# Rotating 96 images by 90 degrees: which bytes of the last group are stored first

## The chip, the core and the metric

The kernel runs on one core of a Trainium2 chip. The metric is the device time of one execution in microseconds (us). Three runs of the kernel before the change took 123.16, 123.51 and 123.54 us, median 123.51.

## What is computed

The input is float32 of shape (32, 3, 256, 256), that is 96 images of 256 x 256, 25.17 MB. The output is each image turned clockwise by a quarter:

```python
def reference(x):
    return np.rot90(x, k=-1, axes=(-2, -1)).astype(np.float32)
```

No arithmetic is done on the values. Every byte is read from device memory (HBM) once and written once, 50.33 MB in all, and between the two it has to change both its partition and its place in the row.

## The kernel before

**Groups.** The 96 images are cut into four groups of 2, 2, 4 and 4 slabs (`sizes`, line 39). A slab is 16 rows of 256 numbers on each of the 128 partitions: 16 KB on a partition, 2 MB in all. Each group has a tile of its own in on-chip memory (`groups`, lines 41 to 44), so no group waits for another's buffer. `E` is the length of a slab's row on a partition, 4096 numbers, `Q` is half of it, and `W` is one image row, 256 numbers.

**Loads.** All loads and stores are DMAs issued by SyncE (SP), in the order of the text. Lines 58 to 69 load the groups in order. The last load is cut in two (lines 66 and 67), and the first of its halves is remembered as `mark`.

**Turning.** VectorE (DVE) transposes with `turn` (line 82): a stream transpose turns blocks of 32 x 32 numbers between partitions and free dimension, and its access patterns, with negative steps, put the reversed order in. ScalarE (ACT) copies with `copy` (line 85). `keep` (line 73) holds the order on each engine as written. A group is turned in place. For that, the output rows of a slab are split in `low` (rows 0 to 7 of its 16, the lower 8 KB) and `high` (rows 8 to 15, the upper 8 KB), and the positions inside a row likewise, which makes four quadrants `A` (low, low), `B_` (high, low), `C_` (high, high) and `D` (low, high), with the row half first (line 118). For groups 2 and 3 there are two turns (t = 0, 1) to a quadrant, and each turn writes its quadrant in all four slabs at once. Quadrant A is first moved aside, so that D, C_ and B_ can be turned into place, and A comes back last.

**The end of the last group** (lines 155 to 171) is what the change concerns. DVE turns A of t = 1 into the side tiles `most` and `spare[0]` (lines 161 and 162). Then come six turns in place (`g3.move`, lines 164 to 166), D, C_ and B_, two of each. With the second B_ turn the rows 8 to 15 of every slab are complete. ACT then brings A of t = 1 back by five copies (lines 167 to 170), and DVE turns A of t = 0 from `spare[1]` into place as its last instruction (line 171). These write rows 0 to 7 of all four slabs; with them the group is complete.

**Waits.** The waits between engines are derived by the framework from which stretches of a tile two instructions touch. In the built program the first store of the last group waits for DVE's semaphore at 25, which DVE's last turn brings it to, and for ACT's at 18.

**Stores.** Lines 174 to 190. Even partitions hold the first half of a group's output rows and odd ones the second (`groups[n][a::2]`), so each group is stored in two halves of 64 partitions, a = 0 and a = 1. A slab's row on a partition is one contiguous stretch of 16 KB in the output. The first store of all waits for `mark`, so that the stores follow the loads. The first half of the last group is stored in three DMAs (lines 185 to 190): the upper 8 KB of slab 0's rows, 512 KB in all, then the lower 8 KB of the same rows, 512 KB, then slabs 1 to 3, 3 MB. The second half is one DMA of 4 MB.

Of the kernel before, what the change touches and what calls it, by code (L numbers as in the profile page):

```python
# [9 lines left out]
def kernel(  # L10
# [14 lines left out]
    nc = tc.nc  # L25
    fp32 = mybir.dt.float32

    B, C, H, W = x.shape
    P = nc.NUM_PARTITIONS
    R = 16  # L30
    E = R * W
    Q = E // 2
# [8 lines left out]
    groups = [  # L41
        ctx.enter_context(tc.tile_pool(name=f"group{n}", bufs=1)).tile([P, s, E], fp32, name=f"u{n}")
        for n, s in enumerate(sizes)
    ]
# [6 lines left out]
    def rows_of(rows, n):  # L51
        return rows[first[n] * P * R : (first[n] + sizes[n]) * P * R]
# [7 lines left out]
    for n in range(1, len(sizes)):  # L60
        I = sizes[n]
# [69 lines left out]
    u = groups[0]  # L131
# [42 lines left out]
    st = rows_of(rows_out, 0).rearrange("(s i m r) w -> i m s (r w)", s=2, i=2, m=P // 2)  # L174
# [5 lines left out]
    for n in range(1, len(sizes)):  # L180
        I = sizes[n]
        st = rows_of(rows_out, n).rearrange("(a i m r) w -> a m i (r w)", a=2, i=I, m=P // 2)
        for a in range(2):
            done = 0
            if (n, a) == (len(sizes) - 1, 0):

                done = 1
                for f in (slice(Q, E), slice(0, Q)):
                    nc.sync.dma_start(out=st[a][:, 0, f], in_=groups[n][a::2, 0, f])
            nc.sync.dma_start(out=st[a][:, done:], in_=groups[n][a::2, done:])  # L190


# [28 lines left out]
```

## Time and profile before

| | |
|---|---|
| three runs, us | 123.16, 123.51, 123.54; median 123.51 |
| the profiled execution, us | 123.7 |
| its span, from the first to the last instruction, us | 121.9 |
| outside the span, us | 1.8 |
| DVE busy | 86.6 us, 71% of the span, 25 instructions |
| ACT busy | 29.1 us, 24% of the span, 20 instructions |
| DMA queue | 50.33 MB, its packets take 97.2% of the 16 DMA engines' span |

A profile shows one execution. "SPq" is SyncE's queue: a DMA_DIRECT2D on it is the issue of one DMA, not its transfer. The transfer is done in packets by 16 DMA engines; in this kernel a packet is one contiguous row of 8, 16 or 32 KB, and each DMA adds one packet of 4 bytes per engine at its end, which signals that it has landed. The share of the DMA engines and the GB/s in the views count these packets.

### The profile page before, as it was taken

The numbers are of one execution on the slowest core, as the hardware profiler recorded it, in microseconds if no ns is written. First come the engines' busy times: TensorE is split into PE (matmuls) and PEld (weight loads), VectorE is DVE, ScalarE is ACT, GpSimd is POOL, SyncE is SP. The second block draws the span as 40 slices with busy tenths as digits, with TensorE's granted clock in tenths as the row PEclk, the third lists the DMA queues.
The fourth block names the chain that finished last, engine by engine and source line by source line (L and its number), as shares of the span: only waits on it lengthen the run. The fifth ranks groups of instructions, "written<-read, shape, count | busy, mean of one in ns | idle before, by whom it ended". The sixth has DMA issues, their size and how long they took to land.

```text
span 121.9 us, 135 instructions
## 1 busy us (share of the span) xinstructions
DVE 86.6 (71%) x25; ACT 29.1 (24%) x20; POOL 0.2 (0%) x4
## 2 busy tenths in 40 slices
DVE  0039999999994199999999999999999960000000
ACT  0000400470005199409462194000003400000000
POOL 0000000000000000000000000000000000000000
DMA  3999999997979898989899999999999989999994
GB/s 86 427 430 427 435 430 430 430 516 344 516 344 516 355 505 376 484 387 473 382 430 430 419 425 414 425 430 430 430 430 430 430 344 430 430 425 425 430 430 183
DMA packets 3264, 50.33 MB, mean 413 GB/s; under 512 B 384, under 2 KB 384, under 8 KB 384
## 3 DMA queue, kind: packets, MB, share of 16 engines
q1 hardware_dynamic: 3264, 50.33, 97.2%
HBM read 25.17 MB, written 25.17 MB: 413 GB/s over the span
## 4 chain that ended last, share of the span: by engine, by line
DVE 44%; DMA 34%; issue 3%; DVEq 0%
DMA u<-in_x_dram 34%; DVE u L82 34%; DVE spare L82 6%; DVE most L82 3%; DVE extra L82 2%; DVEq L82 0%
## 5 line engine op out<-in xcount | busy, mean ns | idle before, releaser
L82 DVE STREAM_TRANSPOSE u<-u 128x2048 f32<-128x2048 f32 x16 | 59.7, 3811 | 0.3
L82 DVE STREAM_TRANSPOSE spare<-u 128x2048 f32<-128x2048 f32 (+1 forms) x4 | 11.9, 2995 | 12.7 <-DMA u<-in_x_dram 12.7
L85 ACT COPY u<-spare 128x512 f32<-128x512 f32 (+2 forms) x8 | 10.5, 1347 | 18.6 <-DVE u L82 13.8
L85 ACT COPY u<-extra 128x1024 f32<-128x1024 f32 (+1 forms) x3 | 5.7, 1937 | 11.1 <-DVE u L82 11.1
L85 ACT COPY u<-most 128x448 f32<-128x448 f32 x4 | 2.1, 563 | 20.4 <-DVE u L82 20.4
L85 ACT COPY spare<-u 128x1024 f32<-128x1024 f32 (+1 forms) x3 | 5.7, 1887 | 2.6 <-DMA u<-in_x_dram 2.6
L85 ACT COPY extra<-u 128x2048 f32<-128x2048 f32 x1 | 4.2, 4234 | 2.5 <-issue 2.5
L85 ACT ACT_TABLE_LOAD x1 | 1.3, 1283 | 13.1 <-DMA u<-in_x_dram 13.1
L82 DVE STREAM_TRANSPOSE extra<-u 128x2048 f32<-128x2048 f32 x1 | 3.9, 3920 | 0.0
L82 DVE STREAM_TRANSPOSE most<-u 128x1792 f32<-128x1792 f32 x1 | 3.6, 3634 | 0.0
L82 DVE STREAM_TRANSPOSE u<-spare 128x2048 f32<-128x2048 f32 x1 | 3.6, 3607 | 0.0
L82 DVE STREAM_TRANSPOSE spare<-spare 128x2048 f32<-128x2048 f32 x1 | 2.3, 2330 | 0.0
L82 DVE STREAM_TRANSPOSE extra<-extra 128x2048 f32<-128x2048 f32 x1 | 2.3, 2311 | 0.0
L205 POOL MEMSET const-bfloat16-1.0<- 128x1 bf16 x1 | 0.1, 101 | 0.0
L205 POOL MEMSET const-uint8-127<- 128x1 uint8 x1 | 0.1, 101 | 0.0
L205 POOL MEMSET const-float32-0.0<- 128x1 f32 x1 | 0.1, 98 | 0.2 <-issue 0.2
L205 POOL MEMSET const-float32-1.0<- 128x1 f32 x1 | 0.1, 98 | 0.0
## 6 DMA issues: line engine op xcount, KB each, us to landing
u<-in_x_dram SPq DMA_DIRECT2D x10, 2048.0 KB, 30.4
out_dram<-u SPq DMA_DIRECT2D x3, 4096.0 KB, 19.4
out_dram<-u SPq DMA_DIRECT2D x4, 2048.0 KB, 13.3
u<-in_x_dram SPq DMA_DIRECT2D x4, 1024.0 KB, 20.4
out_dram<-u SPq DMA_DIRECT2D x1, 3072.0 KB, 10.5
out_dram<-u SPq DMA_DIRECT2D x2, 512.0 KB, 3.3
```

The source lines that it names most:

```text
L82: keep(nc.vector.transpose(out=out, in_=in_))
L85: keep(nc.scalar.copy(out=out, in_=in_))
L205: nc = _bacc.Bacc("TRN2", target_bir_lowering=False, num_devices=1)
```

## The change

Lines 183 to 190 become this. Nothing else differs.

```diff
         for a in range(2):
-            done = 0
+            u = groups[n][a::2]
             if (n, a) == (len(sizes) - 1, 0):
 
-                done = 1
-                for f in (slice(Q, E), slice(0, Q)):
-                    nc.sync.dma_start(out=st[a][:, 0, f], in_=groups[n][a::2, 0, f])
-            nc.sync.dma_start(out=st[a][:, done:], in_=groups[n][a::2, done:])
+                end = Q + 2 * W
+                nc.sync.dma_start(out=st[a][:, I - 1, end:], in_=u[:, I - 1, end:])
+                nc.sync.dma_start(out=st[a][:, : I - 1], in_=u[:, : I - 1])
+                nc.sync.dma_start(out=st[a][:, I - 1, :end], in_=u[:, I - 1, :end])
+            else:
+                nc.sync.dma_start(out=st[a], in_=u)
```

The first half of the last group still leaves in three DMAs. The first is now rows 10 to 15 of slab 3, the upper 6 KB on each of 64 partitions, 384 KB (line 188 of the new kernel). The second is slabs 0 to 2 whole, 3 MB (line 189). The third is rows 0 to 9 of slab 3, 10 KB on each partition, 640 KB (line 190). The second half of the group, and the halves of the other groups, leave as before (line 192). In the built program the 384 KB store waits for DVE's semaphore at 24 alone, which the second B_ turn brings it to, and the 3 MB store waits for DVE's at 25 and ACT's at 19.

## The prediction

> **What bounds the kernel now.** I read the page's slices first, because they tell whether any engine is full for the whole time.
>
> ```profile
> DVE  0039999999994199999999999999999960000000
> DMA  3999999997979898989899999999999989999994
> GB/s 86 427 430 427 435 430 430 430 516 344 516 344 516 355 505 376 484 387 473 382 430 430 419 425 414 425 430 430 430 430 430 430 344 430 430 425 425 430 430 183
> q1 hardware_dynamic: 3264, 50.33, 97.2%
> ```
>
> Each place is 3.05 us. The DMA engines are full nearly throughout, at 97.2% of the span. So the time is the 50.33 MB, plus the stretches in which the DMA engines have nothing to move. Apart from the two ends there is one such place: slice 33 of 40 (97.5 to 100.6 us), with 8 in the row of tenths and 344 GB/s. It lies just where DVE's row ends. The lower values in slices 10 to 20 alternate with values over 500 and only show how packets fall into slices.
>
> Second, the waits of SP's queue and the order of time around that place.
>
> ```profile
> SPq L189 <- DVE u L82: 22.9, 1, 22.9
> ...
> SPq L216 <- DMA out_dram<-u: 18.0, 3, 9.7
> ```
>
> ```profile
> 96.03 3.61 DVE L82 STREAM_TRANSPOSE u<-spare 128x2048 f32<-128x2048 f32 x1
> ...
> 99.71 1.13 SPq L189 DMA_DIRECT2D out_dram<-u  x2
> 100.89 1.99 SPq L190 DMA_DIRECT2D out_dram<-u  x2
> ```
>
> The first store of the last group waits 22.9 us for DVE and is issued at 99.71, right after the last turn ends at 96.03 + 3.61 = 99.64. Everything from there on is store: the end of the program waits for stores only.
>
> Third, slices of 0.2 us there. A packet is booked in the slice in which it starts, so shares can pass 1.
>
> ```profile
> 99.40:99.60 0.20, 0.20 (x1) 0.00 (x0) 0.00 (x0) 1.00 2.90 1229
> 99.60:99.80 0.20, 0.03 (x1) 0.00 (x0) 0.00 (x0) 1.00 0.19 82
> 99.80:100.00 0.20, 0.00 (x0) 0.00 (x0) 0.00 (x0) 1.00 0.00 0
> 100.00:100.20 0.20, 0.00 (x0) 0.00 (x0) 0.00 (x0) 1.00 0.04 0
> 100.20:100.40 0.20, 0.00 (x0) 0.00 (x0) 0.00 (x0) 1.00 0.01 0
> 100.40:100.60 0.20, 0.00 (x0) 0.00 (x0) 0.00 (x0) 1.00 0.00 0
> 100.60:100.80 0.20, 0.00 (x0) 0.00 (x0) 0.00 (x0) 1.00 0.00 0
> 100.80:101.00 0.20, 0.00 (x0) 0.00 (x0) 0.00 (x0) 1.00 1.48 614
> ```
>
> The last packets of group 2 (16 KB, 0.61 to 0.63 us each) start from 99.43 to 99.63 and end, by engine, from 100.05 to 100.24. The first packets of group 3 start from 100.86 to 101.01. So each DMA engine is idle for about 100.86 - 100.05 = 0.81 to 101.01 - 100.24 = 0.77 us, say 0.79. After that they run without a break to 120.75.
>
> **What the change does, part by part.**
>
> *The wait.* The 384 KB store waits for DVE at 24, that is for the second B_ turn, which ends at 96.00, where the last turn starts. Before, the first store waited for the last turn, although the upper 8 KB of slab 0 were complete too. SP stands behind nothing else then: group 2's two stores were issued by 75.30 + 1.40 = 76.70. So the issue moves from 99.71 to about 96.05 and ends near 96.6. What is queued behind it on SP is the 3 MB store, which waits for DVE at 25 and ACT at 19. ACT's last copy ends at 96.96 + 0.36 = 97.32, so DVE's end decides, and the 3 MB store is issued at 99.71 as now. No wait is added for DVE or ACT.
>
> *What fills the gap.* The 384 KB go behind group 2's rows on all 16 engines: 64 rows, 4 to an engine. The trace has no 6 KB row. Its medians are 0.309 us for 8 KB, 0.613 for 16 KB and 1.215 for 32 KB, a straight line, which gives 0.233 us for 6 KB and 0.384 for 10 KB. So each engine has 4 x 0.233 = 0.93 us of work more, from 100.05..100.24 to about 100.99..101.18.
>
> *What is late next: the 3 MB store's first packets.* Two DMAs of this trace start on idle engines. The first load is issued at 0.73, its issue takes 0.42, and its packets start at 1.80, which is 0.65 after the issue ends. The store of line 189 is issued at 99.71, takes 0.494, and its packets start at 100.86, 0.66 after. The issue of a 3 MB store lasted 0.721 (below, first line), and a 4 MB one 0.601 with little queued ahead.
>
> ```profile
> L190 SPq DMA_DIRECT2D out_dram<-u x1: 721/721/721, 100.9 to 100.9; - x1
> ...
> L190 SPq DMA_DIRECT2D out_dram<-u x1: 1301/1301/1301, 60.9 to 60.9; - x1
> ...
> L190 SPq DMA_DIRECT2D out_dram<-u x1: 601/601/601, 74.7 to 74.7; - x1
> ...
> L190 SPq DMA_DIRECT2D out_dram<-u x1: 1397/1397/1397, 75.3 to 75.3; - x1
> ```
>
> With 0.60 to 0.72 its first packets are ready at 99.71 + 0.60 + 0.66 = 100.97 to 99.71 + 0.72 + 0.66 = 101.09, about when the 384 KB run out (100.99..101.18). So a gap of 0 to 0.1 us stays. The bounds: at best the packets are ready 1.15 after the issue starts, as now (100.86), and all 0.79 us go; at worst the issue takes 1.40, the longest in the trace, the packets come at 101.77, the gap that stays is 101.77 - 100.99 = 0.78, and nearly nothing is gained. I take 0.04, since only 64 rows stand ahead of this issue; the issues of 1.30 and 1.40 came behind 256 rows.
>
> *The rest.* Both kernels issue four DMAs for the group and have as many rows and closing packets. The 640 KB and 4 MB issues follow at about 100.5 and 101.0, 6 us or more before the 3 MB are moved, so they are hidden; if that cover were gone they would cost their 0.5 and 1.2 us. Rows of 6 and 10 KB instead of two of 8 KB change nothing on the straight line: 0.233 + 0.384 = 0.617 against 0.618. That is not shown for such rows. Bounds by the nearest rows: if 6 KB cost an 8 KB row and 10 KB a 16 KB row, an engine pays 4 x (0.309 - 0.233) + 4 x (0.613 - 0.384) = 1.22 us more; if 10 KB cost an 8 KB row, 0.30 less. I take 0, as three sizes lie on the line.
>
> *The sum.* -0.79 + 0.04 = -0.75 us. Against the profiled execution's own time, 123.7 us (span 121.9 and 1.8 around it), that is 122.95. That execution was 0.19 above the median of the three runs; against the median it is 123.51 - 0.75 = 122.76, and I give **122.8**.
>
> *A rule against it.* The row: in the present kernel the second 512 KB store and the 3 MB one start their packets on each engine within 0.02 us of the end of the ones ahead of them, so a small DMA costs nothing when it stands behind others. The Trainium skill, "DMA: Bandwidth & Descriptors", section "Rules for kernel authors", asks for 128 partitions and at least 1 MiB per DMA, and its section on the anatomy of one DMA has a fixed part of about 2.0 us for each (fitted there for another way of issuing). If that fixed part were paid in the queue, four DMAs before and four after would make the change worth nothing, by an estimate from that page; by the row it is paid only where the queue is empty.
>
> **Rivals.**
>
> 1. *The gap reopens behind the 384 KB.* The 3 MB store's packets come late, because its issue lasts 1.2 to 1.4 us instead of 0.7. For it: such issues are in the trace. Against it: they had a long queue ahead. Then the packets come at 101.57 to 101.77, the gap that stays is 0.58 to 0.78, and the time is 123.3 to 123.5.
> 2. *The store doesn't leave early*, or its rows wait behind something else. For it: the present kernel's upper half did not leave early either, though its data were there. Against it: the wait is at 24, not 25, in the built program. Then the gap stays and the time is 123.5.
> 3. *Slower: rows of 6 and 10 KB cost what the next larger row costs.* Its place is the four rows of each kind on every engine, in stretches where the engines are the bound; its price up to 1.22 us, so -0.75 + 1.22 = +0.47 and 124.0. It decides from an excess of (0.75 + 0.37) / 8 = 0.14 us a row. For it: no such row in the trace. Against it: 8, 16 and 32 KB are proportional within 2%.
>
> **How the numbers follow.** A difference of 0.3%, 0.37 us, is about what a measurement of this kernel can tell from no change. The forecast has 0.78: a gap of this kind has one cause, and the cause is removed. Rival 1 has 0.12, rival 2 has 0.05, rival 3 has 0.05. The forecast lies under 123.14 but for a little, so faster is 0.77; the same is 0.12 + 0.05 and a little of the forecast's, and less the half of rival 3 that stays small, 0.18; slower is 0.05. The forecast's own range is 122.4, as far below as the lowest of the three runs lies below their median, to 123.1, with 0.3 us of the gap left. The whole range takes in the near end of rival 1 and leaves out its far end and rivals 2 and 3: 122.3 to 123.3.
>
> **What would show it.** In the profile after: the store of line 188 issued near 96.05 and the 3 MB store of line 189 still at 99.71; the slices from 99.8 to 101.0 no longer empty, with 64 packets of 6 KB of about 0.23 us each; the last packet ending at about 120.0 instead of 120.75; a span of 121.1 to 121.2. I am wrong if the issue of line 189 lasts over 1 us, if an empty stretch of more than 0.2 us follows the 6 KB rows, if these rows take over 0.3 us, or if line 188 is issued at 99.7.

## The result, and the profile after

| | before | after |
|---|---|---|
| runs | 22 | 22 |
| median, us | 123.24 | 122.98 |
| lowest to highest, us | 123.11 to 123.62 | 122.78 to 123.46 |
| the profiled execution, us | 123.70 | 122.95 |
| its span, us | 121.9 | 121.2 |

The ratio of after to before is 0.9979, with a 95% interval of 0.9970 to 0.9988: 0.26 us less at the medians, where 0.75 was forecast. The 22 runs of before include the three of the front, whose median was 123.51. The two profiled executions differ by 0.75 us, as forecast, and that is the puzzle of this case: the profile was changed as predicted, the time by a third of it.

The page of the changed kernel, in slices of 3.03 us:

```profile
DVE  0029999999995099999999999999999960000000
DMA  3999999998989898989899999999999999999994
GB/s 84 419 430 433 452 433 427 438 508 357 508 357 508 357 508 357 508 357 508 357 427 433 433 433 433 389 422 406 433 433 433 433 433 427 400 449 454 427 427 184
q1 hardware_dynamic: 3264, 50.33, 97.7%
```

The 8 in the row of tenths at the end of DVE's row (slice 33 of 40) has become a 9, and its 344 GB/s has become 433. The waits of SP's queue in the changed kernel:

```profile
SPq L188 <- DVE u L82: 19.0, 1, 19.0
SPq L218 <- DMA out_dram<-u: 18.1, 3, 9.8
...
SPq L189 <- DVE u L82: 3.1, 1, 3.1
```

The long wait of the last group has been cut in two: the 384 KB store waits 19.0 us for the second B_ turn, and the 3 MB store 3.1 us more for the last turn. The order of time there:

```profile
95.39 0.49 SPq L188 DMA_DIRECT2D out_dram<-u  x1
...
95.40 3.60 DVE L82 STREAM_TRANSPOSE u<-spare 128x2048 f32<-128x2048 f32 x1
...
99.06 0.60 SPq L189 DMA_DIRECT2D out_dram<-u  x1
99.71 0.85 SPq L190 DMA_DIRECT2D out_dram<-u  x1
100.60 1.39 SPq L192 DMA_DIRECT2D out_dram<-u  x1
```

The 384 KB store is issued when the last turn starts, the 3 MB store right after it ends, 0.60 us long, as predicted. But one number does not belong to the change: the last turn starts at 95.40 here and at 96.03 before. Nothing that the change touches comes ahead of it. Slices of 0.2 us, where a packet is booked where it starts:

```profile
99.80:100.00 0.20, 0.00 (x0) 0.00 (x0) 0.00 (x0) 1.00 0.00 0
100.00:100.20 0.20, 0.00 (x0) 0.00 (x0) 0.00 (x0) 1.00 0.63 246
100.20:100.40 0.20, 0.00 (x0) 0.00 (x0) 0.00 (x0) 1.00 0.96 369
100.40:100.60 0.20, 0.00 (x0) 0.00 (x0) 0.00 (x0) 1.00 0.95 369
100.60:100.80 0.20, 0.00 (x0) 0.00 (x0) 0.00 (x0) 1.00 1.19 492
100.80:101.00 0.20, 0.00 (x0) 0.00 (x0) 0.00 (x0) 1.00 1.03 430
101.00:101.20 0.20, 0.00 (x0) 0.00 (x0) 0.00 (x0) 1.00 2.28 963
```

From 100.0 to 101.0, empty before but for its last fifth, the 6 KB rows are moved. The empty slice ahead of them is no gap: the last 16 KB rows of group 2 started at 99.52 to 99.67 and take 0.61 us. The first 6 KB row starts on each engine as group 2's closing packet ends. The rows of the 3 MB store follow at 101.10, with no gap either. The last packet ends at 120.01, against 120.75.

### The profile page after: what moved, and what is told of

It is laid out like the page before. It is cut to its first block, busy times and chain, and to the rows that moved or that the text cites. A ratio compares the mean times of both kernels' runs of the same rounds, so it can differ in the third digit from the quotient of the medians.

```text
span 121.2 us, 134 instructions
## 1 busy us (share of the span) xinstructions
DVE 85.9 (71%) x25; ACT 28.7 (24%) x20; POOL 0.2 (0%) x4
## 4 chain that ended last, share of the span: by engine, by line
DVE 44%; DMA 30%; SPq 4%; issue 3%; DVEq 0%
DVE u L82 33%; DMA u<-in_x_dram 30%; DVE spare L82 6%; DVE most L82 3%; SPq L69 3%; DVE extra L82 2%; SPq L58 1%; SPq L59 0%; DVEq L82 0%
## 5 line engine op out<-in xcount | busy, mean ns | idle before, releaser
L82 DVE STREAM_TRANSPOSE u<-u 128x2048 f32<-128x2048 f32 x16 | 59.0, 3734 | 0.3
L85 ACT COPY u<-spare 128x512 f32<-128x512 f32 (+2 forms) x8 | 10.0, 1292 | 18.2 <-DVE u L82 13.3
```

The costliest lines, as they stand in the source:

```text
L82: keep(nc.vector.transpose(out=out, in_=in_))
L85: keep(nc.scalar.copy(out=out, in_=in_))
```

## The experiments

Three theories were put on record. Theory 1: the gap is as long as DVE's chain happens to end late in an execution, and the profiled execution of before, at 123.70 us slower than all 22 of its runs, had an unusually long one. Theory 2: the gap is 0.8 us in every execution, and the new stores give about 0.5 back. Theory 3: the changed kernel usually has a gap left behind its early rows.

**The kernel before, once more** (b_again; no edit).

> The kernel before, unchanged, profiled and timed once more. Theory 1 (the gap of the DMA engines ahead of the last group is as long as DVE's chain happens to end late; the profiled execution of before, 123.7 us against a median of 123.24, had it longer than most): ratio 1.000, and a profile with a time near 123.2 has DVE's last turn end 0.3 to 0.6 us earlier than 99.64 and a gap of 0.1 to 0.5 us instead of 0.79. Theory 2 (the gap is 0.8 us in every execution, and the new stores give 0.5 us of it back somewhere): the profile has the gap of about 0.79 us again, whatever its time.

Measured: 123.22 us, ratio 0.9989 (0.9978 to 1.0000), so two sets of runs of one kernel can lie 0.1 us apart. The profiled execution took 123.19 us. Its order of time and its slices:

```profile
95.54 3.61 DVE L82 STREAM_TRANSPOSE u<-spare 128x2048 f32<-128x2048 f32 x1
...
99.22 1.13 SPq L189 DMA_DIRECT2D out_dram<-u  x2
```

```profile
100.00:100.20 0.20, 0.00 (x0) 0.00 (x0) 0.00 (x0) 1.00 0.04 0
100.20:100.40 0.20, 0.00 (x0) 0.00 (x0) 0.00 (x0) 1.00 0.69 287
100.40:100.60 0.20, 0.00 (x0) 0.00 (x0) 0.00 (x0) 1.00 0.89 369
```

DVE ends at 99.14, 0.49 earlier than in the first profile, and the first packets of group 3 come at 100.37 instead of 100.86. Group 2's rows end at 99.99 to 100.13, so the gap is 0.36 us as a mean over the engines. From DVE's end to the first packets it is 1.22 us in both profiles, taken before rounding. This is theory 1's picture, not the fixed gap of theory 2.

**DVE later, with the old and the new stores** (b_late, a_late). The same line is added to both kernels ahead of line 171:

```diff
+    turn(out=extra[:, :512], in_=extra[:, :512])
     turn(out=g3.dst[:, 0, low, low], in_=kept.rearrange("p a r g c -> p c r g a"))
```

> The kernel before with one more turn on DVE, 512 numbers of a side tile in place (about 0.58 us), just ahead of the last turn; nothing of the output is left out. Both theories, if the gap is open in every execution: before + 0.58 us, about 123.8. If in some executions DVE is early enough that there is no gap, less than 0.58.

> The changed kernel with the same extra turn of about 0.58 us on DVE. Theory 1: the gap to fill is then about 0.3 + 0.58 = 0.88 us, which the 0.93 us of early rows just hide, so 122.98 + 0.0 to 0.15 us, and the gain over the kernel before with the same turn grows from 0.26 to 0.7 or 0.8. Theory 2: 0.79 + 0.58 - 0.93 = 0.44 us stay open, 123.4, and the gain is 0.4. Theory 3 (the 3 MB store's packets come late in most executions and a gap is left behind the early rows): all of the 0.58 shows, 123.56, and the gain stays at 0.26.

Measured: with the old stores 123.80 us, ratio 1.0034 (1.0022 to 1.0047); with the new ones 123.16 us, 0.9988 (0.9977 to 1.0000). On that chip the kernel before took 123.32 us. The old order pays 0.48 us for the delay of 0.58, less than all of it, as was expected if some executions have no gap. The new one is 0.16 us below before even with it. Between the two the gain has grown from 0.26 to 0.64 us. That is nearest to theory 1's 0.7 to 0.8, and speaks against theory 2's 0.4 and theory 3's 0.26. In the profile of a_late DVE ended at 99.88, and its slices show the cover running out:

```profile
100.80:101.00 0.20, 0.00 (x0) 0.00 (x0) 0.00 (x0) 1.00 0.48 184
101.00:101.20 0.20, 0.00 (x0) 0.00 (x0) 0.00 (x0) 1.00 0.03 0
101.20:101.40 0.20, 0.00 (x0) 0.00 (x0) 0.00 (x0) 1.00 3.08 1311
```

The 6 KB rows end at 100.96 to 101.12, and the 3 MB store's packets start from 101.20 on, 1.32 us after DVE's end: 0.06 to its issue, 0.60 for the issue, 0.66 to the packets. The engines idle for 0.22 us on the mean. Group 2's rows ended at 100.01 to 100.17 there, so with the old stores, whose packets come 1.22 us after DVE's end, that is at 101.10, the gap would have been about 1.0 us. Here the early rows are seen to fill a gap.

**DVE later still, with the new stores** (a_later): the same edit with `extra[:, :1024]`.

> The changed kernel with a turn of 1024 numbers in place on DVE (about 1.2 us) just ahead of the last turn. Theory 1: the early rows hide DVE's end up to about 99.7 us; a typical end of 99.1 + 1.2 is 0.6 past it, so 122.98 + 0.5 to 0.7 us, about 123.6, and the profile has a gap of DVE's end + 1.27 less the end of the 6 KB rows (about 101.05). If the early rows hid any delay, 122.98.

Measured: 123.36 us, ratio 1.0001 (0.9989 to 1.0014): 0.38 us over the 122.98 of the changed kernel in the same session (a_again), where 0.5 to 0.7 was expected. The cover has its end, as theory 1 has it, but the end of DVE that I put in, 99.1 with 1.2 added, was too late by 0.2: in the profile DVE ends at 100.12, where the extra turn moves the last one by 1.12 us. The packets start at 101.44, and the engines idle for 0.35 us.

**DVE earlier, with the old and the new stores** (b_early, a_early, and both again on one chip):

```diff
-    turn(out=g3.dst[:, 0, low, low], in_=kept.rearrange("p a r g c -> p c r g a"))
+    turn(out=g3.dst[:, 0, slice(0, 4), low], in_=kept.rearrange("p a r g c -> p c r g a")[:, :4])
```

> The kernel before with half of DVE's last turn left out (rows 4 to 7 of quadrant A of t = 0 are not written), so that DVE ends about 1.8 us earlier and the stores of the last group are issued while group 2 is still being stored. The gap is gone with the old order and sizes of the stores. Theory 1: the time of the changed kernel, about 122.98 (0.998). Theory 2: 123.24 - 0.79 = 122.45, clearly below the changed kernel, since the new rows' cost is not in it. Theory 3: below the changed kernel too, by what its gap is.

> The changed kernel with half of DVE's last turn left out (rows 4 to 7 of quadrant A of t = 0 are not written), so that DVE ends about 1.7 us earlier. Theory 1: no gap is left to close, so the time of the changed kernel, 122.98, within 0.1 us. Theory 3 (a gap is left in most executions of the changed kernel): faster than that by 0.2 us or more.

Measured: 123.13 us with the old stores, ratio 0.9983 (0.9971 to 0.9995), and 122.88 with the new, 0.9965 (0.9955 to 0.9976), from two chip sessions. Neither profile has a gap. The old order did not fall to theory 2's 122.45, so that theory is out. But the two were 0.25 us apart, which theory 1 does not give, so they were run side by side:

> The kernel before with half of DVE's last turn left out, once more, on the same chip as its counterpart with the changed stores, because the two came out 0.2 us apart in different sessions (0.9983 and 0.9965, intervals that touch). Neither has a gap. Theory 1: the same time as its counterpart, within 0.1 us. Theory 2b (the changed sizes and order of the stores are worth about 0.2 us by themselves, apart from the gap): slower than its counterpart by 0.2 us.

> The changed kernel with half of DVE's last turn left out, once more, as the counterpart. Theory 1: the time of the one with the old stores, both 0.997 to 0.998 of the kernel before. Theory 2b: 0.2 us faster than it.

Measured: 122.92 us with the old stores, ratio 0.9959 (0.9946 to 0.9972), and 122.97 with the new, 0.9959 (0.9944 to 0.9974). Without the gap the two ways of storing take the same time. The 0.25 us between the two sessions did not come back; where it came from was not shown. In the profile of b_early the 16 DMA engines finished 0.48 us apart, in those of the side-by-side runs 0.16 and 0.22.

**The new sizes and order without the early start** (a_held):

```diff
-                nc.sync.dma_start(out=st[a][:, I - 1, end:], in_=u[:, I - 1, end:])
+                tail = nc.sync.dma_start(out=st[a][:, I - 1, end:], in_=u[:, I - 1, end:])
+                tc.add_manual_dep(tail.ins, closing.ins.name, mybir.DependencyInfo(
+                    mybir.DependencyClass.Sync, mybir.DependencyReason.SCHED_ONLY), reason="behind the last turn")
```

Here `closing` is the last turn of line 171.

> The changed kernel with its 384 KB store made to wait for DVE's last turn; sizes, order and number of the stores are those of the change. Theory 1 (all of the gain comes from the rows that leave early; DVE's end decides how much): the time of the kernel before, ratio 0.999 to 1.001, and a gap that is DVE's end + 1.23 us less the end of group 2's rows. Theory 2 (the new rows of 6 and 10 KB cost something of their own): slower than before, up to 1.004.

Measured: 123.20 us, ratio 0.9992 (0.9977 to 1.0006): the kernel before. Rows of 6 and 10 KB cost nothing of their own that these runs can tell, and gain nothing. In its profile DVE ended at 99.92, and the gap was 0.78 us in an execution of 123.93.

**Fewer early rows** (a_3kb):

```diff
-                end = Q + 2 * W
+                end = Q + 5 * W
```

> The changed kernel with the early rows cut to 3 KB (rows 13 to 15 of slab 3, 192 KB), which are 0.47 us of work on each DMA engine. Theory 1 with a typical gap of about 0.33 us: nearly all of the gain stays, 0.997 to 0.998 of the kernel before, and a gap shows only where DVE's last turn ends after about 99.3. If the typical gap were 0.79 as in the profile of before: 0.32 us is left open, which is more than the whole gain, and the time is that of the kernel before or over it.

Measured: 122.91 us, ratio 0.9962 (0.9948 to 0.9976). Half the early bytes keep all of the gain. In the profile a 3 KB row took 0.126 us, so the four rows were 0.50 us of work on an engine, where 0.47 was expected. With a typical gap of 0.79 they could not keep it: 0.29 would have been left.

**The changed kernel, once more** (a_again; no edit).

> The changed kernel once more. Theory 1: ratio 0.997 to 0.999, no gap behind group 2's rows in the profile wherever DVE's end lies up to 99.7, and what is left of the spread of the runs, 0.5 us, is not in this gap. Theory 3: a gap of 0.2 us or more behind the 6 KB rows.

Measured: 122.98 us, ratio 0.9972 (0.9959 to 0.9986), 0.39 us below before's median in that session. In the profiled execution, which took 123.30, DVE ended at 99.20 and there was no gap. Its DMA engines finished between 119.80 and 120.36, on the mean at 119.95, though each had the same bytes as far as the rows can be followed in the trace. In the profile of after, at 122.95 us, they finished between 119.82 and 120.01, on the mean at 119.9. So the 0.35 us between these two executions lie in the engines that finished last. Whether all of the spread that is left comes from this, two profiles do not show.

**Where DVE's delay comes from** (b_nocopy): the kernel before without one copy on ACT.

```diff
-    g2.unline(0, *D, spare[1])
```

> The kernel before without ACT's copy of quadrant D of t = 0 of group 2 from its side tile into place (those numbers are wrong in the output), which ran beside the two turns of DVE at 54.8 and 58.5 us. In the profiles these turns took 3.87 + 3.56 us where the copy took about 3.9, and 4.3 + 4.1 where it took 4.3. Theory 1a (DVE's end varies because these two turns slow down beside the copy, in some executions): the turns take 3.87 + 3.56 or less, DVE ends at 99.1 or earlier, and the runs lose their tail over 123.45. If the transfers of the loads cause it: the turns still vary and the tail stays.

Measured: 123.07 us, ratio 0.9977 (0.9963 to 0.9991), and 122.94 to 123.32 over its 12 runs, where 11 of the 31 runs of before on that chip were over 123.45. Its turn, and the same turn and the copy in the profile of before:

```profile
54.85 3.57 DVE L82 STREAM_TRANSPOSE u<-u 128x2048 f32<-128x2048 f32 x1
```

```profile
54.80 4.30 DVE L82 STREAM_TRANSPOSE u<-u 128x2048 f32<-128x2048 f32 x1
```

```profile
54.92 4.31 ACT L85 COPY u<-spare 128x2048 f32<-128x2048 f32 x1 [4.82 <-DVE spare L82]
```

The first two columns are the start and the duration. Without the copy the turn takes 3.57 us and the next one 3.58. Beside it, in the 13 other profiles of this study, the turn took 3.84 to 4.50, and in four of them 4.2 or more; the next one took 3.56 to 4.21 and was longest in the same four. The late end of DVE in the profile of before comes from here: these two turns took 7.76 us from the first one's start to the start of the turn behind them, and 7.33 in the profile of b_again, 0.43 of the 0.49 us between the two ends, while the rest of DVE's chain took 37.08 and 37.09. DVE ended at 98.97 without the copy and the gap was 0.04 us, so this kernel is faster with the old stores, at the price of numbers left unplaced. There is one profile of b_nocopy; that the slow turns need the copy rests on it and on the 12 times, none over 123.45. Why some executions are slow there and others not stays open.

**The executions together.** The gap and DVE's end are from each profile, the gap as the mean over the 16 engines, from the end of the closing packet to the start of the next row. In a_late and a_later the gap lies behind the 6 KB rows.

| kernel | stores | time, us | DVE's end | gap | time less gap |
|---|---|---|---|---|---|
| before | old | 123.70 | 99.63 | 0.78 | 122.92 |
| b_again | old | 123.19 | 99.14 | 0.36 | 122.83 |
| b_late | old | 123.85 | 99.79 | 0.84 | 123.01 |
| a_held | new, held | 123.93 | 99.92 | 0.78 | 123.15 |
| b_nocopy | old | 123.14 | 98.97 | 0.04 | 123.10 |
| after | new | 122.95 | 99.00 | 0 | 122.95 |
| a_3kb | new, 3 KB | 122.88 | 99.18 | 0 | 122.88 |
| a_late | new | 123.06 | 99.88 | 0.22 | 122.84 |
| a_later | new | 123.32 | 100.12 | 0.35 | 122.97 |
| a_again | new | 123.30 | 99.20 | 0 | 123.30 |

The time less the gap is 122.83 to 123.15 in nine of the ten, whatever the stores. The exception is the execution in which the DMA engines finished 0.56 us apart. The four profiles with half of the last turn left out have no gap and took 122.85 to 123.14.

## Why the prediction came out as it did

- **The wait, the issue and the cover were right.** The 384 KB store left with the second B_ turn (95.39, where DVE's last turn starts at 95.40). The 3 MB store's issue took 0.601 us, at the near end of the 0.60 to 0.72 taken. A row of 6 KB took 0.239 us and one of 10 KB 0.388, against 0.233 and 0.384 from the straight line. The start of packets 0.66 us after an issue ends holds where it can be seen, in a_late: 99.94 + 0.60 + 0.66 = 101.20.
- **Rival 1 did not come**: no gap is left behind the 384 KB while DVE ends before about 99.7 (101.0 less 1.32). It is the right picture for the executions with DVE made later. **Rival 2** was built in a_held and is the kernel before, as priced. **Rival 3** is out, by a_held and by the row times, which give 4 x (0.239 + 0.388 - 2 x 0.309) = 0.04 us an engine where it had up to 1.22. The long issues that rival 1 feared do occur, 0.85 and 1.39 us for the 640 KB and 4 MB stores, where 6 us of rows cover them.
- **The sum against the profiled execution came out, but by luck**: 123.7 - 0.75 = 122.95, and the profiled execution after took 122.95. DVE ended 0.63 us earlier in that execution, at 99.00. With the old stores the first packets would have come at about 99.00 + 1.22 = 100.22, and group 2's rows ended at 100.13 to 100.30, so there was hardly a gap left to fill; b_nocopy, with the old stores and DVE's end at 98.97, had 0.04. That the early rows do fill a gap is shown by a_late and by the times, not by this pair of profiles.
- **The step that failed is the term of -0.79 us, carried over to the median**: "against the median it is 123.51 - 0.75 = 122.76". The 0.79 was the gap of one execution, and its length is DVE's end + 1.22 us less the end of group 2's rows. The profiled execution was 0.46 us above the median of the 22 runs. If that excess is itself a longer gap, the median execution has a gap of about 0.79 - 0.46 = 0.33 us, and that is what the change can give: measured were 0.26 and 0.39 in two sessions. The profile of b_again, an execution near the median, has a gap of 0.36. The text saw that the execution was 0.19 above the median of three runs and still took the whole gap off that median. A sign was in the profile: the turns at 54.8 and 58.5 took 4.30 and 4.05 us, where the eight turns of the same shape behind them took 3.57 to 3.90.
- **The rule that was weighed.** The Trainium skill, "DMA: Bandwidth & Descriptors", asks for at least 1 MiB per DMA in "Rules for kernel authors". Here stores of 384 KB and of 192 KB, put behind others, cost the time of their rows alone: the 3 MB store's rows started within 0.01 us of the closing packets ahead of them. The row decided rightly.

The gain is below the 0.3% that the prediction named as what a measurement can tell from no change, so by that measure what came is "the same", to which it gave 0.18, where it gave 0.77 to faster. 22 runs tell the gain, at 0.12 to 0.30%, and a_again, in another session, has 0.28%.

## What to carry to other kernels

A gap in a profile belongs to one execution. Before a saving is taken off the median, set the profiled execution's own time against the median: the excess may be that same gap, and then the median has only the rest of it to give. Where a full transfer queue runs dry between two groups, a small transfer that is ready early closes the gap, and it needs no more bytes than the gap is long.

## What the runs showed of the hardware

A turn on DVE and a copy on ACT that ran beside each other slowed down together: the turn took 3.84 to 4.50 us beside the copy and 3.57 without it, the copy 4.31 us in the profile of before and 3.88 in that of after. Both write the same tile, and the copy reads another memory (`spare` is in PSUM); which of the things that they share it is was not tried, nor were the loads that ran at the same time taken away. The Trainium skill, "SBUF — State Buffer", section "SBUF: two separate sides", says that ACT's port and DVE's dedicated pair of ports do not wait on anyone; these runs do not show a wait at a port, but the two engines were not independent here.

A DMA issued on idle engines started its packets 0.65 to 0.66 us after the issue ended, so 64 rows (issue 0.494 us) start earlier than three slabs (0.601 us): 1.22 us after DVE's end against 1.32.
